# Two halved weight differences, two later roundings, weights' work ahead of finished tiles, and the last squares summed on VectorE

## The chip, the cores and the metric

The kernel runs on one core of a Trainium2 chip. The metric is device time in microseconds (us) of one execution. Five engines run beside each other, each in its own program order: TensorE (PE, with its weight loads PEld), VectorE (DVE), ScalarE (ACT), GpSimd (POOL) and SyncE (SP), which here only issues transfers. They hand work to one another by semaphores.

## The reference

A decoder trunk of two layers on 1024 tokens of width 1024, batch 1, all in float32. Layer 0 mixes tokens with a recurrent block (RG-LRU), layer 1 with stick-breaking attention; each mixer is followed by a feed-forward part with `D_FF` = 2816. What is computed around the change:

```python
def rms_norm(x, g):
    xf = x.astype(jnp.float32)
    y = xf * lax.rsqrt(jnp.mean(xf * xf, axis=-1, keepdims=True) + RMS_EPS)
    return (y * g.astype(jnp.float32)).astype(x.dtype)

def swiglu_ffn(x, w_in, w_out):
    gu = jnp.einsum("bsd,df->bsf", x, w_in)
    h = jax.nn.silu(gu[..., :D_FF]) * gu[..., D_FF:]
    return jnp.einsum("bsf,fd->bsd", h, w_out)

    # per layer
    hn = rms_norm(h, mix_norm[layer])
    h = h + mixed                      # the mixer's output for hn
    h = h + swiglu_ffn(rms_norm(h, ffn_norm[layer]), ffn_w_in[layer], ffn_w_out[layer])
    # after both layers
    return rms_norm(h, final_norm)
```

## The kernel before

**Operands in two parts.** To keep float32 accuracy each operand is split into a high part, rounded by ScalarE to TensorE's `fp32r` format, and a low part, the difference, made by VectorE. One matrix product is then three matmuls (lines 142 to 144): high weights by high data, high weights by low data, low weights by high data. A low part of the weights is so first read by the third matmul of a product.

**Layout.** Activations lie transposed: tile `h[d][n]` holds 128 of the 1024 features (d is 0 to 7) by 512 of the 1024 tokens (n is 0 or 1).

**Seven products.** The feed-forward parts are done by a Strassen-like scheme: a 2 by 2 block product with seven smaller products instead of eight, in the order `ORDER = (0, 1, 2, 3, 4, 6, 5)`. The seven weight operands are made from the raw weights by VectorE sums (`s12`, `s2`, `s3`, `do_s4`) and splits: `a_hi`/`a_lo` (tiles `wah`, `wal`, products 0 and 1), `b_hi`/`b_lo` (`wbh`, `wbl`, products 2 and 4), `c_hi`/`c_lo` (`wch`, `wcl`, products 3 and 5), `d_hi`/`d_lo` (`wd`, product 6). The `_hi` step is on ScalarE, the `_lo` step on VectorE. The seven products lie in three PSUM banks: products 0, 2, 4 and 5 share one, 3 and 6 another. A product that comes on top of an earlier one in its bank (`onto`) may start only after the earlier one has been copied out.

**Steps.** A loop over `steps` runs first 21 "f" steps (columns of `ffn_w_in`, results gated by SiLU and stored through memory) and then the 13 "v" steps, the *visits* of `ffn_w_out`: visit (d, p0, p1) adds pairs p0 to p1 of the inner features to the four tiles of features d and d+4. Visits 9 to 12 are the last for d = 1, 2, 3, 0. Inside a step the loop index `k` runs over the seven products. After each product, in program order: `post` or `post_out` takes the product from PSUM (products 0, 2, 3 and 4 of a visit by a ScalarE copy, line 1176, and then a VectorE add or subtract, lines 1178 and 1180; the others by VectorE straight from PSUM); then the tiles that the product before has finished are worked up by `finished`; then the weight work of this and of the next step (`c_hi`, `c_lo` at k = 0; `d_hi`, `d_lo`, the next step's `a_hi` at 2; its `s12` at 3; `a_lo`, `s2`, `s3` at 4; `b_hi`, `do_s4` at 5). `b_lo` opens the next step. A prologue (lines 993 to 1022) computes column 0 and makes the weights of step 1.

**What `finished` does.** In layer 0 (not `final`) it stores the tile, splits it for the next mixer (`prep`: ScalarE line 220, VectorE line 221) and squares it for the next norm (`squares`: ScalarE line 216, sum by VectorE line 217). In layer 1 (`final`) it squares the tile on ScalarE (line 216; the first square of each n goes straight into `acc[n]`, line 213), adds the square on GpSimd (line 217), and scales the tile by the final norm's gain on ScalarE (line 227). The square goes through `rbc[n]`, one buffer for each n. `finish` (from line 1386) then runs visit 12 of layer 1 for single tiles, sums the squares by matmuls with a column of ones (`stats`, line 206), and transposes, scales and stores the output.

**Roundings of the visits' data.** The moving operands of the visits come back from memory in one part and are split by `split_op` (ScalarE line 1113, VectorE line 1114). A list `tasks` says after which product of the last f step (0 to 6) or of the first visit (7 is its first product) each split is issued:

```python
tasks = [(at, p, i) for at, i in zip((2, 2, 3, 4, 5, 5, L), ORDER) for p in range(2)]
```

**Order.** In both feed-forward blocks the order on TensorE, ScalarE, VectorE and GpSimd is the order of the code (`manual_schedule`); only SyncE's queue is ordered by the planner there. In the attention all five queues follow the code.

Of the kernel before, what the change touches and what calls it, by code (L numbers as in the profile page):

```python
# [33 lines left out]
def trunk(  # L34
# [21 lines left out]
    nc = tc.nc  # L56
    f32 = lambda t: t.bitcast(F32)
# [40 lines left out]
    rbc = [cp.tile([P, NB], F32, name=f"rbc{n}") for n in range(NH)]  # L98
    acc = [None] * NH
# [12 lines left out]
    def load_raw(src, shape):  # L112
        raw = rp.tile([P, D], F32, tag="raw", name="raw")
        view = raw if len(shape) == 1 else raw.rearrange("p (a b) -> p a b", a=shape[0])
        nc.sync.dma_start(view, src)
        return raw
# [33 lines left out]
    def wtile(nm):  # L150
        return wpool[0].tile([P, D], F32R, tag="w", name=nm)
# [59 lines left out]
    def squares(h, d, n, sqp, acc, eng=None, first=None):  # L211
        if d == 0 if first is None else first:
            nc.scalar.square(acc[n], h[d][n])
        else:
            sq = sqp[n % len(sqp)] if isinstance(sqp, list) else sqp.tile([P, NB], F32, tag="sq", name="sq", bufs=2)
            nc.scalar.square(sq, h[d][n])
            (eng or nc.gpsimd).tensor_add(acc[n], acc[n], sq)

    def prep(h, d, n, gcol):
        nc.scalar.activation(xh[d][n], h[d][n], AF.Copy, scale=vc[:, gcol + d : gcol + d + 1])  # L220
        nc.vector.scalar_tensor_tensor(
            xl[d][n], h[d][n], vc[:, gcol + d : gcol + d + 1], f32(xh[d][n]), op0=ALU.mult, op1=ALU.subtract
        )


    def gain(h, d, n):
        nc.scalar.activation(h[d][n], h[d][n], AF.Copy, scale=vc[:, V_FIN + d : V_FIN + d + 1])
# [31 lines left out]
    with ExitStack() as st, tc.manual_schedule(engines={E.PE, E.Activation, E.DVE, E.Pool, E.SP}):  # L259
# [95 lines left out]
        for ks in (range(4), range(4, ND)):  # L355
            for lhs, rhs in ((0, xh), (0, xl), (1, xh)):
                for k in ks:
                    first, last = lhs == k == 0 and rhs is xh, lhs == 1 and k == ND - 1
# [35 lines left out]
    with ExitStack() as st:  # L394
        lp = st.enter_context(tc.tile_pool(name="lp", bufs=1, reuse_waits="tile"))
        psl.append(lst.enter_context(tc.tile_pool(name="psB", bufs=2, space=PSUM, reuse_waits="tile")))
        V = nc.vector
        lam = vc[:, V_LAM : V_LAM + ND]
        sm = lambda name: lp.tile([P, ND], F32, name=name)
        V = nc.vector  # L400
# [164 lines left out]
    ORDER = (0, 1, 2, 3, 4, 6, 5)  # L565
    BANK = {0: 0, 2: 0, 4: 0, 5: 0, 1: 1, 3: 2, 6: 2}
    HK = ND // 2
# [57 lines left out]
    def mix_out_ffn_in(mix, bias, layer, gnext, outs):  # L625
        w_in = ffn_w_in[layer]
        gcol = V_FFN + layer * ND
        V = nc.vector
# [5 lines left out]
        v, h = {}, []  # L634
# [10 lines left out]
        if outs:  # L645
# [6 lines left out]
            class Six:  # L652
                at = 0
# [14 lines left out]
        class Weights:  # L668
# [14 lines left out]
            def part(self, t, x):  # L683
                return half(t, x)[:, 0 : self.m * P]
# [22 lines left out]
                self.wa = wtile("wah")  # L707
                nc.scalar.copy(self.full(self.wa), self.full(self.ra))

            def a_lo(self):  # L710
                lo = wtile("wal")
                V.tensor_sub(self.full(lo), self.full(self.ra), self.full(f32(self.wa)))
                self.put((0, 1), self.wa, lo)

            def b_hi(self):
# [38 lines left out]
        def weights_in(f, now=True):  # L754
            w = Weights(lambda x: load_raw(cols(w_in, x * DFF + f * P), (ND,)))
            if now:
                w.load_a()
                w.load_b()
            return w
# [11 lines left out]
        with tc.manual_schedule(engines={E.PE, E.Activation, E.DVE, E.Pool}):  # L771
# [12 lines left out]
            for j in range(HK):  # L784
                rows = (j, j + HK)
                dn = [(d, n) for d in rows for n in range(NH)] if j else [(d, n) for n in range(NH) for d in rows]
                for k, (d, n) in enumerate(dn):
                    o = HK * j + k
                    if (d, n) in begun:
                        ps = begun[d, n]  # L790
                        hi, lo = mix.w[d]
# [24 lines left out]
                    elif o == 14:  # L816
                        w.b_hi()
                        w.b_lo()
                        nw = weights_in(1)
# [28 lines left out]
            def post0(i, ps):  # L848
                g0, g1, u0, u1 = halves(0)
                if i == 0:  # L850
                    nc.scalar.copy(g1, ps)
                elif i == 1:
                    V.tensor_add(g0, ps, g1)
                elif i == 2:
                    V.tensor_add(g1, ps, g1)
                elif i == 4:
                    V.tensor_add(u0, ps, g1)
                elif i == 3:
                    V.tensor_sub(u1, u0, ps)
                    V.tensor_sub(g1, g1, ps)  # L860
                elif i == 5:
                    V.tensor_add(u0, ps, u0)
                else:
                    V.tensor_sub(g1, g1, ps)
# [131 lines left out]
            for k, i in enumerate(ORDER0[:6]):  # L996
                part(P0[i], w, i, rhs_in[i], (HK - 1,))
                if k == 1:
                    w.d_hi()
                    w.d_lo()  # L1000
                elif k == 3:
                    nw.a_hi()
                elif k == 5:
                    nw.a_lo()
                if k < 5:
                    post0(i, P0[i])
            ps = half(ob, 0)
# [107 lines left out]


            L = NPROD
            tasks = [(at, p, i) for at, i in zip((2, 2, 3, 4, 5, 5, L), ORDER) for p in range(2)]

# [28 lines left out]


            begun_sq, last_sq = set(), []
            done = []

            def finished(d, n):
                if final:
                    squares(h, d, n, rbc, acc, first=n not in begun_sq)
                    gain(h, d, n)
                else:
                    nc.sync.dma_start(hd[d][n], h[d][n])  # L1160
                    prep(h, d, n, gnext)
                    if d in (VISITS[-1][0], VISITS[-2][0], VISITS[-1][0] + HK, VISITS[-2][0] + HK):
                        last_sq.append((d, n))
                    else:
                        squares(h, d, n, acc, rbc, V, first=n not in begun_sq)
                begun_sq.add(n)
# [25 lines left out]
            for s_, (kind, x) in enumerate(steps):  # L1192
                w, nw, ahead = nw, nxt, None
# [23 lines left out]
                for k, i in enumerate(ORDER):  # L1217
# [18 lines left out]
                    if not final and kind == "v" and x == NV - 1:  # L1236
                        if k == 0:
                            raw = load_raw(cols(w_qkv, 0), (ND,))
                        elif k == 4:
                            qh = ring.four.tile([P, D], F32R, tag="w", name="whi")  # L1240
                            nc.scalar.copy(qh, raw)
                        elif k == 5:
                            ql = ring.four.tile([P, D], F32R, tag="w", name="wlo")
                            V.tensor_sub(ql, raw, f32(qh))
                            k3 = lambda t: t.rearrange("p (k c) -> p k c", k=ND)
                            wq0.append((k3(qh), k3(ql)))
                    if i == 1 and even:
                        ga, gb = (q4(halves(x)[0], y) for y in range(2))
                        V.tensor_add(ga, I[0], ga)
                        V.tensor_add(ga, I[1], ga)  # L1250
                        inner_w()
                    elif i == 1 and odd:
                        ha, hb = (q4(halves(x)[0], y) for y in range(2))
                        V.tensor_sub(gb, gb, I[3])
                        V.tensor_add(ha, I[0], ha)
                        V.tensor_add(hb, I[0], hb)
                        V.tensor_sub(hb, hb, I[2])
                        V.tensor_add(ha, I[1], ha)
                    elif kind == "f":
                        post(x, i, banks[b])  # L1260
                        if i == 3 and even:
                            V.tensor_sub(gb, gb, I[2])
                            V.tensor_add(gb, I[0], gb)
                    else:
                        old = done[:]
                        del done[:]
                        post_out(x, i, banks[b])
                        for dn in old:
                            finished(*dn)
                    if s_ == 0:  # L1270
                        if k < 2:
                            for _ in range(2):
# [6 lines left out]
                    if k == 0:  # L1279
                        if kind == "v":  # L1280
                            w.c_hi()
                        w.c_lo()
                    elif k == 2:
                        w.d_hi()
                        w.d_lo()
                        if nw:
                            nw.a_hi()
                    elif nw and last_two:
                        if k == 4:
                            nw.a_lo()  # L1290
                            nw.r_hi()
                        elif k == 6:
                            nw.r_lo()
                    elif nw:
                        if k == 3:
                            nw.s12()
                        elif k == 4:
                            nw.a_lo()
                            nw.s2()
                            nw.s3()  # L1300
                        elif k == 5:
                            nw.b_hi()
                            nw.do_s4()
                    soon = kind == "f" and x + 1 in PAIRS
                    if soon and k == 3:
                        inner_sums(nw.ra, ahead.ra)
# [63 lines left out]
                        open_last()  # L1370
            for dn in done:
                finished(*dn)
            last_sq.sort(key=lambda t: t[1])
            for k, (d, n) in enumerate(last_sq):
                nc.scalar.square(acc[k % NH], h[d][n])
# [102 lines left out]
    with ExitStack() as st:  # L1478
# [261 lines left out]
        with tc.manual_schedule(engines={E.PE, E.Activation, E.DVE, E.Pool, E.SP}):  # L1740
# [3 lines left out]
            first = qkv_steps(0)  # L1744
# [20 lines left out]
            c = 0  # L1765
# [84 lines left out]
```

## Time and profile before

| what | value |
|---|---|
| median of three runs (lowest, highest) | 2173.48 us (2171.96, 2173.48) |
| time of the profiled execution | 2172.33 us |
| its span, first to last instruction | 2170.6 us |
| ScalarE busy | 1110.1 us (51%) |
| VectorE busy | 1777.2 us (82%) |
| GpSimd busy | 122.0 us (6%) |

The time of an execution is 1.7 us more than the span of its trace. Stretches that the text speaks of, in us from the span's start:

| stretch | where |
|---|---|
| 333 to 343 | prologue of layer 0's feed-forward part (1542 in layer 1) |
| 746, 1946 | last f step to visit 0, layer 0 and layer 1 |
| 932 | visit 10 to visit 11, layer 0 |
| 954 | layer 0's last visit to the first q/k/v product |
| 2129 | visit 10 to visit 11, layer 1 |
| 2144.5 to 2170.6 | `finish` |

A line of the timeline reads: start (us), length (us), engine, source line, operation, output tile <- input tiles, shapes, count, and in brackets how long the engine had been idle and for whom it waited. A line of the waits reads: engine, tile and line <- the engine and line waited for: us in total, times, longest. Lines of grouped instructions give a count and shortest, median and longest duration in ns.

### The profile page before, as it was taken

Reading aid. Unit: us, or ns where it says so; the run is one execution under the profiler, and the core shown is the slowest. Engines: PE = TensorE matmul, PEld = TensorE weight load, DVE = VectorE, ACT = ScalarE, POOL = GpSimd, SP = SyncE. Lnnn points to the kernel's source line nnn. Section 1 sums busy time; section 2 is a strip of 40 time slices with the busy share of each in tenths; the row PEclk is TensorE's granted clock in tenths of the full one; section 3 lists DMA queues with packets and bytes.
Section 4 is the critical chain, followed back from the end, with each engine's and each line's share of the span. In section 5 each row is a group of like instructions: output and inputs, shape, how many; then the busy total and the mean of one; then the engine's idle time right before and its main releaser. Section 6 shows DMA issues by size and latency. Waiting matters only on the chain.

```text
span 2170.6 us, 28348 instructions
## 1 busy us (share of the span) xinstructions
PE 2157.1 (99%) x10414; PEld 1812.1 (83%) x10414; DVE 1777.2 (82%) x2604; ACT 1110.1 (51%) x1821; POOL 122.0 (6%) x85
## 2 busy tenths in 40 slices
PE   8999999999999999999999999999999999999998
PEld 7888888888888888888888888888888888888887
DVE  7888778888888887887888888876888888888886
ACT  6577445444444544554555555553544444454556
POOL 1222020000000000000000000012000000000002
PEclk9999999999999999999999999999999999999999
DMA  7111422334445864434333344553133444587442
GB/s 234 49 49 39 163 87 72 107 126 160 134 149 201 267 222 130 146 119 104 99 97 93 95 105 107 147 202 119 60 120 113 153 141 156 176 276 232 136 154 89
DMA packets 305323, 294.49 MB, mean 136 GB/s; under 512 B 16280, under 2 KB 212000, under 8 KB 305184
## 3 DMA queue, kind: packets, MB, share of 16 engines
q1 hardware_dynamic: 305024, 292.42, 42.8%
q8 instruction: 81, 1.33, 0.2%
q14 instruction: 58, 0.48, 0.1%
q10 hardware_dynamic: 160, 0.27, 0.0%
HBM read 184.09 MB, written 83.36 MB: 123 GB/s over the span
## 4 chain that ended last, share of the span: by engine, by line
PE 97%; DVE 2%; ACT 1%; issue 0%; DMA 0%; DVEq 0%; ACTq 0%
PE p_ps L144 17%; PE p_ps L142 17%; PE p_ps L143 17%; PE qk_ps L142 4%; PE qk_ps L144 4%; PE qk_ps L143 4%; PE wt_ps L1654 3%; PE a_ps L143 3%; PE a_ps L144 3%; PE a_ps L142 3%; PE ob_ps L143 3%; PE ob_ps L142 3%; PE ob_ps L144 2%; PE z_ps L1620 2%; PE av_ps L1676 2%; PE z_ps L1621 2%
## 5 line engine op out<-in xcount | busy, mean ns | idle before, releaser
L142 PE MATMUL p_ps<-vh,wbh 128*128 128x512 f32 x524 | 204.8, 391 | 0.0
L143 PE MATMUL p_ps<-vl,wbh 128*128 128x512 f32 x524 | 204.5, 390 | 0.0
L144 PE MATMUL p_ps<-vh,wbl 128*128 128x512 f32 x524 | 204.2, 390 | 0.2 <-DVE wbl L721 0.2
L142 PE MATMUL p_ps<-vh,wch 128*128 128x512 f32 x524 | 204.2, 390 | 0.0
L144 PE MATMUL p_ps<-vh,wcl 128*128 128x512 f32 x524 | 204.1, 390 | 0.0
L143 PE MATMUL p_ps<-vl,wch 128*128 128x512 f32 x524 | 203.9, 389 | 0.0
L717 ACT CAST wbh<-sb 128x1024 fp32r<-128x1024 f32 (+2 forms) x69 | 69.6, 1008 | 191.6 <-DVE sb L701 191.6
L1633 ACT ACTIVATE w<-z_ps 128x128 f32<-128x128 f32 (+1 forms) x192 | 94.1, 492 | 143.1 <-PE z_ps L1621 143.0
L144 PE MATMUL p_ps<-vh,wal 128*128 128x512 f32 x396 | 154.3, 390 | 0.1
L143 PE MATMUL p_ps<-vl,wah 128*128 128x512 f32 x396 | 154.1, 389 | 0.0
L142 PE MATMUL p_ps<-vh,wah 128*128 128x512 f32 x396 | 154.1, 389 | 0.0
L1664 DVE TENSOR_TENSOR tl<-wt_ps,th 128x512 fp32r<-128x512 f32 x192 | 97.9, 552 | 68.0 <-ACT th L1663 67.9
L144 PEld LDWEIGHTS p_ps<-vh,wbl 128*128 128x128 f32 x524 | 98.4, 188 | 22.3 <-DVE wbl L721 1.5
L144 PEld LDWEIGHTS p_ps<-vh,wcl 128*128 128x128 f32 x524 | 98.4, 188 | 21.1 <-DVE wcl L731 0.6
L142 PEld LDWEIGHTS p_ps<-vh,wch 128*128 128x128 f32 x524 | 98.4, 188 | 20.4 <-ACT tb L1176 0.2
L143 PEld LDWEIGHTS p_ps<-vl,wch 128*128 128x128 f32 x524 | 98.4, 188 | 20.4
L142 PEld LDWEIGHTS p_ps<-vh,wbh 128*128 128x128 f32 x524 | 98.6, 188 | 19.2 <-ACT ta L1176 0.2
L143 PEld LDWEIGHTS p_ps<-vl,wbh 128*128 128x128 f32 x524 | 98.6, 188 | 18.6
L142 PE MATMUL qk_ps<-vh,whi 128*128 128x512 f32 x264 | 111.2, 421 | 0.0
L1640 DVE TENSOR_TENSOR_SCAN w<-w,unit 128x128 f32<-128x128 f32 (+3 forms) x128 | 103.7, 816 | 4.6 <-ACT w L1633 4.3
L144 PE MATMUL qk_ps<-vh,wlo 128*128 128x512 f32 x264 | 103.7, 393 | 0.0
L143 PE MATMUL qk_ps<-vl,whi 128*128 128x512 f32 x264 | 103.4, 392 | 0.0
(390 smaller groups left out, 5896.4 us busy)
## 6 DMA issues: line engine op xcount, KB each, us to landing
raw<-in_ffn_w_in SPq DMA_DIRECT2D x88, 512.0 KB, 3.9
vl<-pd SPq DMA_DIRECT2D x128, 256.0 KB, 3.5
pd<-U SPq DMA_DIRECT2D x90, 256.0 KB, 2.3
kk<-two SPq DMA_DIRECT2D x64, 256.0 KB, 4.1
raw<-in_ffn_w_out SPq DMA_DIRECT2D x56, 256.0 KB, 3.6
raw<-in_attn_w_qkv SPq DMA_DIRECT2D x24, 512.0 KB, 4.0
h<-hd SPq DMA_DIRECT2D x32, 256.0 KB, 5.4
hd<-h SPq DMA_DIRECT2D x32, 256.0 KB, 2.0
```

What stands on the lines that cost most here:

```text
L142: nc.tensor.matmul(ps, lhsT=wh, rhs=mh, start=first, stop=False, **kw)
L143: nc.tensor.matmul(ps, lhsT=wh, rhs=ml, start=False, stop=False, **kw)
L144: nc.tensor.matmul(ps, lhsT=wl, rhs=mh, start=False, stop=last, **kw)
L717: nc.scalar.copy(self.full(self.wb), self.full(self.sb))
L1620: nc.tensor.matmul(ps[:, 0 : c1 - c0], lhsT=lhsT, rhs=KK[q][hx][:, 0, c0:c1], start=True, stop=False)
L1621: nc.tensor.matmul(ps[:, 0 : c1 - c0], lhsT=lhsT, rhs=KK[q][hx][:, 1, c0:c1], start=False, stop=True)
L1633: nc.scalar.activation(F, ps[:, 0:n], AF.Sigmoid, scale=-SC)
L1640: nc.vector.tensor_tensor_scan(rev, rev, unit[:, NB - n :][:, ::-1], 0.0, op0=ALU.mult, op1=ALU.add)
L1654: nc.tensor.transpose(tp[:, c : c + P], W[q, hx, j, kb // 4][:, (kb % 4) * P : (kb % 4 + 1) * P], ident)
L1664: nc.vector.tensor_sub(tl[:, q0:], tp[:, q0:], f32(th)[:, q0:])
L1676: nc.tensor.matmul(ps[:, q0:], lhsT=VV[q][:, kb, hx], rhs=tl[:, q0:], start=False, stop=last)
```

## The change

Four things are edited. `a_lo` gets a form that makes `wal` by two instructions of half the width, used once in each prologue, and the first low q/k/v weights `wlo` at the end of layer 0 are made in two instructions, feature tiles 1, 2, 5, 6 first and 0, 3, 4, 7 second. The splits for product 6 move from after the sixth product of the last f step (5) to after the first of visit 0 (`L`, 7), those for product 5 from there to one product later. `finished` moves behind the weight work of the same product. In layer 1 the sums of squares go from GpSimd to VectorE, a product after the square (`add_up`).

```diff
-            def a_lo(self):
+            def a_lo(self, parts=1):
                 lo = wtile("wal")
-                V.tensor_sub(self.full(lo), self.full(self.ra), self.full(f32(self.wa)))
+                if parts == 1:
+                    V.tensor_sub(self.full(lo), self.full(self.ra), self.full(f32(self.wa)))
+                else:
+                    for x in range(2):
+                        V.tensor_sub(self.part(lo, x), self.part(self.ra, x), self.part(f32(self.wa), x))
                 self.put((0, 1), self.wa, lo)
...
                 elif k == 5:
-                    nw.a_lo()
+                    nw.a_lo(2)
...
-            tasks = [(at, p, i) for at, i in zip((2, 2, 3, 4, 5, 5, L), ORDER) for p in range(2)]
+            tasks = [(at, p, i) for at, i in zip((2, 2, 3, 4, 5, L, L + 1), ORDER) for p in range(2)]
...
-            done = []
+            done, to_add = [], []
+
+            def add_up():
+                while to_add:
+                    n = to_add.pop(0)
+                    V.tensor_add(acc[n], acc[n], rbc[n])
 
             def finished(d, n):
                 if final:
-                    squares(h, d, n, rbc, acc, first=n not in begun_sq)
+                    if n in begun_sq:
+                        nc.scalar.square(rbc[n], h[d][n])
+                        to_add.append(n)
+                    else:
+                        nc.scalar.square(acc[n], h[d][n])
                     gain(h, d, n)
...
                             ql = ring.four.tile([P, D], F32R, tag="w", name="wlo")
-                            V.tensor_sub(ql, raw, f32(qh))
                             k3 = lambda t: t.rearrange("p (k c) -> p k c", k=ND)
+                            ka = lambda t: t.rearrange("p (a k c) -> p a k c", a=2, k=HK)
+                            for y in (slice(1, 3), slice(0, HK, HK - 1)):
+                                V.tensor_sub(ka(ql)[:, :, y], ka(raw)[:, :, y], ka(f32(qh))[:, :, y])
                             wq0.append((k3(qh), k3(ql)))
...
                         post_out(x, i, banks[b])
-                        for dn in old:
-                            finished(*dn)
                     if s_ == 0:
...
                             nw.b_hi()
                             nw.do_s4()
+                    if kind == "v":
+                        add_up()
+                        for dn in old:
+                            finished(*dn)
                     soon = kind == "f" and x + 1 in PAIRS
...
             for dn in done:
                 finished(*dn)
+                add_up()
             last_sq.sort(key=lambda t: t[1])
```

## The prediction

> **What bounds the kernel now.** First the page's engine rows, then PEld's waits, then the timeline of each place that is edited.
>
> ```profile
> PE 2157.1 (99%) x10414; PEld 1812.1 (83%) x10414; DVE 1777.2 (82%) x2604; ACT 1110.1 (51%) x1821; POOL 122.0 (6%) x85
> ```
> ```profile
> PEld p_ps L144 <- DVE wbl L721: 1.5, 3, 0.7
> PEld p_ps L144 <- DVE wal L712: 1.0, 2, 0.5
> ...
> PEld p_ps L142 <- ACT ta L1176: 0.7, 2, 0.5
> PEld p_ps L144 <- DVE wcl L731: 0.6, 2, 0.4
> ...
> PEld qk_ps L144 <- DVE wlo L1244: 0.4, 1, 0.4
> ```
>
> TensorE is the bound everywhere, so an edit pays only where TensorE waits. All waits that the edits can reach are these 4.2 us of its weight loads. How much of such a wait TensorE itself loses is read from the first prologue:
>
> ```profile
> 342.61 0.39 PE L142 MATMUL p_ps<-vh,wah 128*128 128x512 f32 x1
> 342.84 0.39 PE L143 MATMUL p_ps<-vl,wah 128*128 128x512 f32 x1
> 343.29 0.50 PE L144 MATMUL p_ps<-vh,wal 128*128 128x512 f32 x1
> 343.63 0.40 PE L142 MATMUL p_ps<-vh,wah 128*128 128x512 f32 x1
> ```
>
> Matmuls start 0.23 apart; here one comes 0.45 after its predecessor and the next 0.34 after that. So 0.22 is lost to the wait and 0.11 to picking up again, 0.33 of a wait that the list counts as 0.5: two thirds. The 4.2 us are therefore worth 2.8 us at most, 0.13% of the kernel, and whatever the change adds is set against that.
>
> **Halves of `wal`: -0.7.** The difference starts too late for the third matmul of step 1:
>
> ```profile
> 342.02 1.22 DVE L712 TENSOR_TENSOR wal<-raw,wah 128x1024 fp32r<-128x1024 f32 x1
> ```
>
> The first half, which alone product 0 reads, takes the 0.69 of a 512-wide VectorE row (below) and ends at 342.71, before the 343.07 at which the third matmul is due. The second is read 12 matmuls after 342.61, at 345.3, and is there by 343.4. Both waits go: two thirds of 1.0. Two instructions for one keep VectorE 0.06 longer (starts 0.60 apart, twice, for 1.14), which no wait behind it sees.
>
> **Halves of `wlo`: -0.3.** The q/k/v product begins with features 1, 5, 2, 6, which the first half holds; the second half has some 12 matmuls of cover. Two thirds of 0.4.
>
> **Roundings two products later: +0.1 in all.** Before visit 0 of layer 1 (and alike in layer 0):
>
> ```profile
> 1943.13 2.50 DVE L1114 TENSOR_TENSOR vl<-vl,vh 128x512 fp32r<-128x512 f32 x4
> 1945.54 0.69 DVE L721 TENSOR_TENSOR wbl<-sb,wbh 128x512 fp32r<-128x512 f32 x1
> ...
> 1949.81 0.43 DVE L740 TENSOR_TENSOR wd<-s,wd 128x256 fp32r<-128x256 f32 x1
> ```
> ```profile
> 1944.53 0.59 ACT L1176 COPY U<-p_ps 128x512 f32<-128x512 f32 x1 [0.23 <-PE p_ps L144]
> ```
> ```profile
> 1946.29 0.50 PE L144 MATMUL p_ps<-vh,wbl 128*128 128x512 f32 x1
> ...
> 1950.54 0.39 PE L144 MATMUL p_ps<-vh,wd 128*128 128x512 f32 x1
> ```
>
> Two of the four splits leave the place ahead of `wbl`, which starts 1.2 earlier; its wait (0.4 of the 1.5 in each layer) goes, -0.27 a layer. They then stand with the two of product 5 ahead of `wd`. VectorE cannot use the whole 1.2, as its next instruction needs the copy that ends at 1945.12: it starts at 1945.15 instead of 1946.14, 1.0 earlier. Two splits of 0.60 more come behind it, so `wd` ends at 1950.24 + 0.2 = 1950.45. TensorE, 0.25 earlier without the first wait, wants it at 1950.29. It loses 0.05 (from a result to its reader, 1946.23 to 1946.29 at `wbl`) + 0.16 + 0.11 = 0.32. Net +0.05 a layer; bounds -0.27 (the end of `wd` is hidden) to +0.3.
>
> **Weights ahead of finished tiles, layer 0: +0.2.** `finished` now waits behind `b_hi` on ScalarE, which itself waits for the sums:
>
> ```profile
> 929.20 0.84 ACT L717 CAST wbh<-sb 128x768 fp32r<-128x768 f32 x1 [0.56 <-DVE sb L701]
> ```
> ```profile
> 933.28 0.96 DVE L721 TENSOR_TENSOR wbl<-sb,wbh 128x768 fp32r<-128x768 f32 x1
> ```
> ```profile
> 934.46 0.39 PE L144 MATMUL p_ps<-vh,wbl 128*128 128x512 f32 x1
> ```
>
> ScalarE is then free for visit 10's tile (6, 1) at 929.94 (0.74 after `b_hi` starts) and has split it 0.72 later, at 930.66. VectorE, which went straight from the take-over of product 6 (done at 929.68) to that tile, has only the short sum `do_s4` (0.47) to do meanwhile and stands still from 930.15 to 930.70. All behind inherits the 0.55: `wbl` starts at 933.83 and ends at 934.79. TensorE wants it at 934.46: 0.38 with the hand-over, and 0.11 to pick up, +0.49. In return `wcl` of visit 11 no longer stands behind tile (6, 0): its wait of 0.4 goes, -0.27. Bounds: -0.27 to +0.5. Before visit 10 the same move is hidden (the VectorE instruction ahead of `wbl` waits for TensorE), before visit 12 there are no squares. The stores of finished tiles on SyncE's queue wait for the tile alone, and its loads run two steps ahead: nothing.
>
> **Sums on VectorE, layer 1: +1.8.** What they replace:
>
> ```profile
> L217 POOL TENSOR_TENSOR acc<-acc,rbc x30: 1289/1302/1747, 274.1 to 2146.2; 128x512 f32<-128x512 f32 x30
> L217 DVE TENSOR_TENSOR acc<-acc,rbc x8: 684/686/689, 348.7 to 1551.5; 128x512 f32<-128x512 f32 x8
> ```
> ```profile
> 2128.33 1.66 DVE L701 TENSOR_TENSOR sb<-raw 128x384 f32<-128x384 f32 x1
> ...
> 2132.18 1.93 DVE L721 TENSOR_TENSOR wbl<-sb,wbh 128x768 fp32r<-128x768 f32 x1
> 2134.03 1.79 DVE L1180 TENSOR_TENSOR g<-ta,g 128x512 f32<-128x512 f32 x1
> ```
> ```profile
> 2131.28 0.63 ACT L216 ACTIVATE rbc<-g 128x512 f32<-128x512 f32 x1 [0.42 <-DVE g L1178]
> 2131.95 0.73 ACT L227 ACTIVATE g<-g,vc 128x512 f32<-128x512 f32 x1
> 2132.57 0.57 ACT L1176 COPY ta<-p_ps 128x512 f32<-128x512 f32 x1
> ```
> ```profile
> 2133.22 0.48 PE L142 MATMUL p_ps<-vh,wbh 128*128 128x512 f32 x1
> ```
>
> Ten sums of 1.3 on GpSimd become ten of 0.69 on VectorE. The gain: beside GpSimd's sum `wbl` takes 1.93, in layer 0 0.96; without it the waits for `wbl` (0.7) and for the copy `ta` (0.7) could go, 0.9 in all. The loss: squares of tiles with the same n share `rbc[n]`. At the end of visit 10 the tiles (6, 1) and (2, 1) come one product apart. The second square must wait for the first's sum, and that now stands on VectorE behind the take-over of the last product. VectorE reaches that take-over, which stood 0.60 ahead of `wbl`, at 2131.07 instead of 2131.58: `s3` (line 701) no longer takes 1.66 beside GpSimd but some 0.55, less one sum of 0.60 put in. The sum runs from 2131.67 to 2132.36, the square starts at 2132.42, the gain follows 0.67 later and the copy of product 0 of visit 11 another 0.63 later, at 2133.72 instead of 2132.57; it ends at 2134.31. Product 2 lies on product 0's bank and was due at 2133.22: it starts at 2134.37, +1.15, and +0.11. It lost some 0.6 around `wbl` already and product 6 0.3 at `ta`, both of which go (ScalarE has caught up by product 3). TensorE enters `finish` 0.15 late at this point.
>
> There the same hand-over meets the norm:
>
> ```profile
> 2144.73 0.69 DVE L1180 TENSOR_TENSOR g<-p_ps,g 128x512 f32<-128x512 f32 x1 [1.36 <-PE p_ps L144]
> ```
> ```profile
> 2146.85 1.28 ACT L1438 ACT_TABLE_LOAD   x1
> 2148.14 0.20 ACT L1438 ACTIVATE rcol<-ones 128x1 f32<-128x1 f32 x1
> ```
> ```profile
> 2151.56 0.69 DVE L1408 TENSOR_TENSOR acc<-acc,rbc 128x512 f32<-128x512 f32 x1 [0.70 <-ACT rbc L1406]
> ```
> ```profile
> 2152.48 0.61 PE L206 MATMUL st_ps<-ones,acc 128*128 128x1 f32 x5
> ```
>
> From the last take-over T (2144.73) to `stats` there are 7.75. Now: take-over and `wrl` 0.60 each, sum of (7, 1) 0.75 with its hand-over, then on ScalarE square and gain of (3, 1) and of (7, 0), 2 x (0.67 + 0.63), table 1.28, root 0.11: `finish`'s first square starts at T + 5.94. Square 0.66, its sum 0.60, the second tile's take-over 0.75, its square 0.70, its sum 0.75: `stats` at T + 9.40, 1.65 late. With the 0.15: +1.8, and nothing behind `stats` gives it back, since TensorE's transposes follow in order. Bounds: -0.9 (all hidden) to +3.1 (one more late copy, 1.26). I take 1.8, as every length is from a row of the same 20 us.
>
> A page of the Trainium skill would make this longer: "ScalarE: Activation LUTs", section "What ACT_TABLE_LOAD costs", gives 1.28 us for the load and about 1.38 us for a drain with each switch of sets. The row has the 1.28, and the root starts at its end, with no drain in sight; by the page's figure the term would be an estimated +3.2 and the total +2.5.
>
> **Sum.** -0.7 - 0.3 + 0.1 + 0.2 + 1.8 = +1.1 us. The execution profiled took 2172.33 (span 2170.6 and 1.7 around it): 2173.4. The median, 2173.48, is 1.15 above that execution, so I forecast 2174.6, no change that this kernel's measurement can tell (0.2%, 4.3 us).
>
> **The rivals.** *The gains alone.* If ScalarE's late copy and `finish`'s sums are covered after all, nothing is lost: -2.8, 2170.7. For it: every wait of the list is on a moved or shortened instruction. Against: one `rbc[n]`, and 0.2 between the end of the sum that `stats` reads (2152.25) and `stats`. *The halves don't count.* If a reader waits for the whole tile, the 1.0 of the halves is not won: 2175.6. Against: `wcl` is made and read in halves already. *The late copy again.* Products 3 and 4 of visit 11 wait for their copies like product 0, another 1.26 each: 2177.1. For it: `ta` and `tb` are in the wait list. Against: by product 3 ScalarE has 0.6 to spare. *A slower table switch.* If the switch first lets the last square and gain run out, 1.30 is added to the chain in `finish`: 2175.9. Against: the load's row starts where the last gain ends (2146.85). (A drain as on the Trainium skill's "ScalarE: Activation LUTs" would be such a wait.) *The other side: the clock falls.* TensorE's granted clock:
>
> ```profile
> 2169.00:2170.00 1.00, 0.00 (x0) 0.00 (x0) 0.00 (x0) 0.00 (x0) 0.00 (x0) 0.61 0.02 4
> ```
>
> The last matmul ends near 2165; four us later the clock, 1.00 until then, drops. If the wait at 2133 or at `stats` let it drop, TensorE's remaining 13 to 31 us would run at half speed: up to as much again, 2187 to 2205. It decides from a wait of about four us. Against: my longest is 1.65. (The Trainium skill, "TensorE: Matmul & The Clock Gate", "What's actually happening", puts the limit at one idle window of about 3.4 us; by that rule too the clock stays.)
>
> **How the numbers follow.** Forecast 0.46; gains alone 0.19; halves don't count 0.10; late copy again 0.13; table switch 0.05; clock 0.07. The forecast's own bounds: 2172.9 to 2176.5. The range goes down to 2170.5 and up to 2177.3, which leaves out the clock, half of the late copy and some of the gains. Slower by over 0.2% (above 2177.8) are the clock and 0.06 of the late copy, where it comes with the upper bounds of the other terms: 0.13. Faster by over 0.2% (below 2169.1) is more than all waits are worth: 0.03, for waits that I don't see. The rest, 0.84, is within 0.2%.
>
> **What would show it.** Right: no wait of PEld for `wal` and `wlo`; no 1.93 on `wbl`; before visit 11 of layer 1 a wait for the copy `ta` of about 1.2; `stats` starting 9.4 after the last take-over, with a wait for VectorE's `acc`; a short wait for `wd` in visit 0 and for `wbl` before visit 11 of layer 0. Wrong: ScalarE's copy of product 0 on time, or `stats` without a wait. A drop of the granted clock before 2165 would be the last rival.

## The result and the profile after

The changed kernel takes 2176.32 us (median of 22 runs, 2173.55 to 2177.0), the kernel before on the same chips 2172.84 (22 runs, 2171.85 to 2174.35): a ratio of 1.0015, with an interval of 1.0009 to 1.0022. It is 3.5 us slower, inside the range that I gave and 1.7 above the forecast, still within the 0.2% of "same". The profiled execution took 2176.84 us, its span is 2175.1.

The engine row of the page, and the list of PEld's waits (us in total, times, longest):

```profile
PE 2159.7 (99%) x10414; PEld 1815.5 (83%) x10414; DVE 1780.3 (82%) x2617; ACT 1109.3 (51%) x1821; POOL 107.1 (5%) x75
```
```profile
PEld st_ps L206 <- DVE acc L1426: 1.7, 1, 1.7
...
PEld p_ps L142 <- ACT ta L1189: 1.3, 1, 1.3
...
PEld p_ps L144 <- DVE wd L744: 0.7, 2, 0.3
PEld p_ps L144 <- DVE wbl L725: 0.7, 1, 0.7
...
PEld st_ps L206 <- DVE rbc L1394: 0.5, 1, 0.5
```

`wal`, `wlo` and `wcl` are gone from the list. In their place stand `acc` at `stats`, one long wait for the copy `ta`, two short ones for `wd`, one for `wbl` (layer 0), and two kinds that I had not named: for `rbc` at another `stats`, and three for a copy `G` (0.9 in all, 0.3 before).

Since TensorE issues the same matmuls in the same order in both kernels, I laid the two traces side by side and noted each place where the distance between a matmul's two starts changes. A step includes what TensorE loses in picking up again behind a wait, some 0.1. Steps below 0.05 are left out; the others add up to the difference of the spans to within 0.1:

| place (us in the trace before) | predicted | measured |
|---|---|---|
| start-up, to 13 us | - | +1.25 |
| 343, 1542: halves of `wal` | -0.33 each | -0.34 each |
| 746, 1946: `wbl` no longer waits | -0.27 each | -0.25 each |
| 751, 1951: product 6 late | +0.32 each | +0.30 each |
| 934: `wbl` late, layer 0 | +0.49 | +0.51 |
| 937: `wcl` no longer waits, layer 0 | -0.27 | -0.23 |
| 955: halves of `wlo` | -0.3 | -0.26 |
| 966: second `stats` of the attention | none | +0.30 |
| 2133 to 2141: visit 11, layer 1, net | +0.15 | +0.15 |
| 2152: `stats` in `finish` | +1.65 | +1.74 |
| 2154 to 2158: granted clock | none | +1.58 |
| total | +1.1 | +4.5 |

The first row is no effect of the edits. The 16 transposes that open both traces are unchanged:

```profile
9.55 1.96 PE L316 MATMUL tp<-ident,xt 128*128 128x128 f32 x16 [1.47 <-DVE hc L323]
```
```profile
9.70 3.65 PE L316 MATMUL tp<-ident,xt 128*128 128x128 f32 x16 [1.69 <-DMA xt<-in_x]
```

The first row is of the kernel before, the second of the changed one: there this execution met TensorE at half speed for longer. In the traces of the experiments this step goes either way, from -0.8 to +1.6, which fits runs of one kernel that differ by 2 us or more. Without it 3.2 of the 4.5 us are left, and the medians differ by 3.5.

**The +0.30 at 751 and 1951 is two waits.** In the changed kernel near 1951:

```profile
1946.62 2.18 ACT L1117 CAST vh<-vl 128x512 fp32r<-128x512 f32 x4
...
1950.22 0.59 ACT L1189 COPY G<-p_ps 128x512 f32<-128x512 f32 x1
...
1950.86 0.50 PE L142 MATMUL p_ps<-vh,wd 128*128 128x512 f32 x1
...
1951.50 0.50 PE L144 MATMUL p_ps<-vh,wd 128*128 128x512 f32 x1
```

The moved splits have a half on ScalarE too. It now rounds four tiles at once where it had rounded two (2.18 for 1.14), its next copies are late, and product 6 waits for the copy `G` that ends at 1950.81: 0.03 and 0.11 for picking up. The difference `wd` costs 0.08 and 0.11.

**The two large steps are where the prediction had put them.** Visit 10 to visit 11 of layer 1, from the timeline of the changed kernel:

```profile
2132.72 0.68 DVE L1162 TENSOR_TENSOR acc<-acc,rbc 128x512 f32<-128x512 f32 x1
2133.32 0.95 DVE L725 TENSOR_TENSOR wbl<-sb,wbh 128x768 fp32r<-128x768 f32 x1
...
2133.43 0.63 ACT L1167 ACTIVATE rbc<-g 128x512 f32<-128x512 f32 x1 [0.74 <-DVE acc L1162]
2134.10 0.72 ACT L227 ACTIVATE g<-g,vc 128x512 f32<-128x512 f32 x1
2134.73 0.56 ACT L1189 COPY ta<-p_ps 128x512 f32<-128x512 f32 x1
...
2135.34 0.50 PE L142 MATMUL p_ps<-vh,wbh 128*128 128x512 f32 x1 [0.91 <-ACT ta L1189]
```

The sum (line 1162) frees `rbc`; only then does ScalarE, 0.74 idle, start the second square, then the gain, then the copy for which TensorE stands still. And `wbl` takes 0.95 instead of 1.93, as GpSimd works on nothing beside it. In `finish`:

```profile
2145.89 0.69 DVE L1193 TENSOR_TENSOR g<-p_ps,g 128x512 f32<-128x512 f32 x1 [1.35 <-PE p_ps L144]
...
2150.49 1.28 ACT L1456 ACT_TABLE_LOAD   x1
2151.79 0.20 ACT L1456 ACTIVATE rcol<-ones 128x1 f32<-128x1 f32 x1
...
2154.54 0.69 DVE L1426 TENSOR_TENSOR acc<-acc,rbc 128x512 f32<-128x512 f32 x1 [0.69 <-ACT rbc L1424]
...
2155.28 1.05 PE L206 MATMUL st_ps<-ones,acc 128*128 128x1 f32 x8 [1.48 <-DVE acc L1426]
```

From the last take-over (2145.89) to `stats` (2155.28) there are 9.39 us. I had worked out 9.40.

**What I had not expected follows from that wait.** Three stretches of 3.41 us, the first beginning where TensorE's last matmul ahead of the wait ends (length, then busy time of PE and the other engines, then the granted clock, PEclk):

```profile
2153.80:2157.22 3.42, 1.94 (x18) 1.94 (x18) 1.91 (x8) 2.43 (x5) 0.00 (x0) 1.00 0.00 0
2157.22:2160.63 3.41, 3.41 (x19) 3.41 (x17) 2.50 (x6) 2.26 (x4) 0.00 (x0) 0.50 0.31 117
2160.63:2164.04 3.41, 3.41 (x33) 3.41 (x33) 1.57 (x8) 1.92 (x5) 0.00 (x0) 1.00 0.51 191
```

In the first TensorE is idle for 1.48. In the second, back at work, it is granted half its clock: 19 matmuls instead of some 33. In the third the clock is whole again. Half of 3.41 is 1.71, and the matmuls fall back 1.58.

### The profile page after: what moved, and what is told of

Read it like the earlier page. It is cut to its first block, busy times and chain, and to the rows that moved or that the text cites. A ratio compares the mean times of both kernels' runs of the same rounds, so it can differ in the third digit from the quotient of the medians.

```text
span 2175.1 us, 28346 instructions
## 1 busy us (share of the span) xinstructions
PE 2159.7 (99%) x10414; PEld 1815.5 (83%) x10414; DVE 1780.3 (82%) x2617; ACT 1109.3 (51%) x1821; POOL 107.1 (5%) x75
## 4 chain that ended last, share of the span: by engine, by line
PE 97%; DVE 1%; ACT 1%; DMA 0%; issue 0%; SPq 0%; DVEq 0%
PE p_ps L142 17%; PE p_ps L143 17%; PE p_ps L144 17%; PE qk_ps L142 4%; PE qk_ps L144 4%; PE qk_ps L143 4%; PE wt_ps L1672 3%; PE a_ps L143 3%; PE a_ps L144 3%; PE a_ps L142 3%; PE ob_ps L144 3%; PE ob_ps L143 3%; PE ob_ps L142 3%; PE z_ps L1638 2%; PE av_ps L1694 2%; PE z_ps L1639 2%
```

## The experiments

Four questions were open: whether the shared square buffer, rather than VectorE's load, makes the chain late; whether the clock falls because of the wait at `stats`, and from what length; where the 0.30 at 966 comes from; and what the order in layer 0 costs.

### Who pays for the late sums

**The sums back on GpSimd**, all else as changed:

```diff
-                    if n in begun_sq:
-                        nc.scalar.square(rbc[n], h[d][n])
-                        to_add.append(n)
-                    else:
-                        nc.scalar.square(acc[n], h[d][n])
+                    squares(h, d, n, rbc, acc, first=n not in begun_sq)
```

> The changed kernel with layer 1's sums of squares back on GpSimd; halves, roundings and the order of the finished tiles stay as changed. Theory (the sums on VectorE make the late copy before visit 11 and the wait at stats, and that wait lets the clock fall): no wait of the stats matmuls for acc, granted clock 1.00 until the end, about 1.6 + 1.7 us less than the changed kernel, near 2173.0, the same as the kernel before within 0.5 us. Rival (it is the moved order, not the sums): the wait at stats and the half clock stay, 2175.5 or more.

**The sums on VectorE, each square in a buffer of its own** (four free halves of the `UT` tiles in turn), all else as changed:

```diff
-                    n = to_add.pop(0)
-                    V.tensor_add(acc[n], acc[n], rbc[n])
+                    n, sq = to_add.pop(0)
+                    V.tensor_add(acc[n], acc[n], sq)
...
-                        nc.scalar.square(rbc[n], h[d][n])
-                        to_add.append(n)
+                        sq = half(UT[1 + n_sq[0] // 2 % 2], n_sq[0] % 2)
+                        n_sq[0] += 1
+                        nc.scalar.square(sq, h[d][n])
+                        to_add.append((n, sq))
```

> The changed kernel, sums still on VectorE, but each square goes to one of four buffers of its own, so that no square waits for an earlier sum. Theory (the hand-over through one rbc[n] is what costs): no wait of about 1.1 for the copy ta before visit 11, wait at stats under 0.3, clock 1.00: 1.1 + 1.6 + 1.7 less than the changed kernel, near 2171.9, about 1 us faster than the kernel before. Rival (VectorE has too little room for ten more sums): at least half of the wait at stats stays, clock falls as before, 2175 or more.

GpSimd: 2172.19 us (2170.89 to 2172.97, 11 runs), 0.9994 of the kernel before (0.9985 to 1.0003). Own buffers: 2172.07 (2170.77 to 2172.86, 11 runs), 0.9991 (0.9982 to 1.0000). After 2125 us the list of PEld's waits has one line in each, and none for `stats`; first GpSimd's, then that of the own buffers:

```profile
PEld p_ps L142 <- ACT ta L1185: 0.7, 1, 0.7
```
```profile
PEld p_ps L142 <- ACT ta L1191: 0.5, 1, 0.5
```

In both traces the granted clock stays at 1.00 to the last matmul, and visit 11 is a gain: -0.48 net with GpSimd, which fits that kernel's coming out lower than expected, and -0.69 with own buffers, where the changed kernel has +0.15. These are steps of single traces, and the kernel before does not lose the same there each time: in one of the experiments below (the second trace with two subtractions, whose visit 11 is unedited) it is 0.61 faster. There GpSimd's sum took 2.82 instead of 1.75, and VectorE's line 701 beside it 0.55 instead of 1.66. VectorE does the same ten sums in the second kernel as in the changed one, and the wait at `stats` is gone. So it is not their load that cost the time, but one buffer handed to and fro between two engines that each work in order. Ten sums on VectorE with room for the squares are as good as ten on GpSimd; the two kernels cannot be told apart.

### What makes the clock fall

**TensorE kept busy ahead of `stats`**, by matmuls into a PSUM bank whose result nothing reads; first twelve of 256 columns, later six of 512 (the diff is of the six):

```diff
-        rest = last(1, *mid, ahead=lambda: stats(acc[0], pp, "p", 0))
+        def filled():
+            ps = pp.tile([P, NB], F32, tag="p", name="st_ps")
+            for _ in range(FILL):
+                nc.tensor.matmul(ps, lhsT=w.a[0][0][:, 0:P], rhs=R[p0][0][0], start=True, stop=True)
+            for i in range(4):
+                nc.tensor.matmul(ps[:, i : i + 1], lhsT=acc[0][:, i * P : (i + 1) * P], rhs=ones, start=True, stop=True)
+            rstd(rcol[:, 0:4], ps[:, 0:4])
+
+        rest = last(1, *mid, ahead=filled)
```

> The changed kernel with twelve matmuls of 256 columns (about 1.4 us) put ahead of the stats matmuls, into unused columns, so that TensorE works through most of its wait. Theory (the idle time lets the clock fall): stats starts where it did, the granted clock stays 1.00 until the end, 1.7 us less than the changed kernel, near 2174.6. Rival (the clock falls for what follows, the many small matmuls and transposes, and not for the wait): half clock for some 3.4 us after stats all the same, 2176.3.

> The changed kernel with six 512-wide matmuls on a spare PSUM bank put on TensorE ahead of `stats` (nothing reads them), so that TensorE does not stand still while it waits for the sum. It repeats the twelve narrower ones with half as many instructions. Theory (the clock falls because TensorE stood still at `stats`): clock 1.00 to the last matmul, and the time is the changed kernel's less 1.7: 0.9993 of it, about 1.0007 of the kernel before (2174.6). Rival (the clock falls because the eight narrow matmuls come late, whatever stands before them): half clock for some 3.4 us stays, 1.0015. With half the extra instructions the last stores should land as early as in the changed kernel; if what delayed them with twelve fillers comes again, the trace ends about 1.9 later than its last matmul says, 1.0009 or more.

Twelve: 2175.73 us (2174.94 to 2176.69, 11 runs), 1.0009 (1.0000 to 1.0018). Six: 2175.34 (2174.53 to 2176.45, 11 runs), 1.0008 (0.9999 to 1.0017). With six, the stretch with the wait and the one behind it:

```profile
2152.83:2156.25 3.42, 3.33 (x24) 2.73 (x22) 1.97 (x6) 2.43 (x5) 0.00 (x0) 1.00 0.00 0
2156.25:2159.66 3.41, 3.41 (x33) 3.41 (x32) 2.71 (x9) 2.11 (x4) 0.00 (x0) 1.00 0.29 109
```

TensorE is idle for 0.09 and the clock stays whole. `stats` is as late as in the changed kernel (+1.64), yet behind it only the 0.10 for picking up is lost. By the ratios the kernel with matmuls that do nothing is 0.0007 faster than the changed one, some 1.5 us, where 1.7 had been expected. The intervals of 1.0008 and 1.0015 overlap, so the traces carry this, not the times. With twelve the trace shows the same, but its last stores landed 1.8 later than the last matmul led one to expect. With six they did not, and the times of the two kernels cannot be told apart, which fits a matter of that one execution. What it was stays open.

**The same wait without the change**: the kernel before, with idle subtractions on VectorE ahead of the sum that `stats` reads.

```diff
                 nc.scalar.square(sq, t)
+                if (x, n, i0) == (1, 0, 0):
+                    for _ in range(DOSE):
+                        nc.vector.tensor_sub(rows[4][:, 0:NB], sq, t)
                 if add:
```

> The kernel before with one idle VectorE subtraction (0.60) put ahead of the sum that `stats` reads, nothing else. `stats` waits some 0.4 us. Theory (a still TensorE ahead of `stats` lets the clock fall, from some length between 0.4 and 1.5 us): no fall here, +0.4 to +0.5, ratio 1.0002. Rival (any wait there lets it fall): +2.1, 1.0010.

> As with one subtraction, but two: `stats` waits some 1.0 us. If the clock falls the time is +1.1 and another 1.7, 1.0013; if not, +1.1, 1.0005. The theory leaves this length open.

> As before, but three: `stats` waits some 1.6 us, as long as in the changed kernel. Theory (the length of the stand-still does it, whatever the change is): half clock for some 3.4 us from two us after the wait, +1.6 and +1.7 = +3.3, ratio 1.0015. Rival (the clock falls in the changed kernel for another reason, such as what its earlier waits did): +1.6 alone, 1.0007.

> The kernel before with two idle VectorE subtractions ahead of the sum that `stats` reads, a second look at the same kernel. The granted clock changes on a grid of 3.41 us, and in the first look the stand-still of 0.99 lay across a boundary of it (0.71 and 0.28). If the still share of one stretch of the grid decides, a look in which all 0.99 lie in one stretch may fall to half clock for the next; if 0.99 is too short whatever its place, the clock stays at 1.00.

One subtraction: 2174.21 us, 1.0003 (0.9995 to 1.0012). Two: 2175.41, 1.0010 (1.0002 to 1.0019). Three: 2176.68, 1.0015 (1.0006 to 1.0024); 11 runs each. With three, as in the changed kernel, the clock falls, here for two stretches on end:

```profile
2151.32:2154.73 3.41, 1.69 (x15) 1.49 (x13) 2.91 (x5) 1.12 (x2) 0.00 (x0) 1.00 0.00 0
2154.73:2158.15 3.42, 3.42 (x17) 3.42 (x18) 1.40 (x8) 1.19 (x3) 0.00 (x0) 0.50 0.00 0
2158.15:2161.56 3.41, 3.41 (x18) 3.41 (x17) 2.05 (x4) 2.19 (x4) 0.00 (x0) 0.50 0.33 124
```

So it is the wait ahead of `stats` that does it, whatever made it. Two traces of the kernel with two subtractions show how. `stats` waits 0.99 both times. The first trace:

```profile
2151.18:2154.60 3.42, 2.69 (x22) 2.46 (x20) 2.47 (x4) 0.94 (x2) 0.00 (x0) 1.00 0.00 0
2154.60:2158.01 3.41, 3.15 (x28) 3.15 (x29) 2.45 (x10) 2.18 (x5) 0.00 (x0) 1.00 0.00 0
2158.01:2161.42 3.41, 3.41 (x33) 3.38 (x32) 2.19 (x6) 2.60 (x7) 0.00 (x0) 1.00 0.60 224
```

And the second trace of the same kernel:

```profile
2154.30 1.05 PE L206 MATMUL st_ps<-ones,acc 128*128 128x1 f32 x8 [0.99 <-DVE acc L1411]
...
2152.96:2156.38 3.42, 2.43 (x21) 2.22 (x21) 2.60 (x8) 1.80 (x4) 0.00 (x0) 1.00 0.00 0
2156.38:2159.79 3.41, 3.41 (x18) 3.41 (x17) 2.35 (x6) 2.19 (x4) 0.00 (x0) 0.50 0.40 150
```

The stretches are on a grid: every change of the clock within a trace lies a whole number of 3.41 us from the others. In the first trace the grid cuts the idle time into 0.73 and 0.26, and the clock stays. In the second all 0.99 lie in one stretch, and the next one runs at half clock: 1.57 lost. Where the grid lies differs from one execution to the next.

### The 0.30 at 966, and layer 0's order

**`wlo` whole again**, all else as changed:

```diff
+                            V.tensor_sub(ql, raw, f32(qh))
                             k3 = lambda t: t.rearrange("p (k c) -> p k c", k=ND)
-                            ka = lambda t: t.rearrange("p (a k c) -> p a k c", a=2, k=HK)
-                            for y in (slice(1, 3), slice(0, HK, HK - 1)):
-                                V.tensor_sub(ka(ql)[:, :, y], ka(raw)[:, :, y], ka(f32(qh))[:, :, y])
```

> The changed kernel with `wlo` at the end of layer 0 made in one piece again. Theory (the halves' gain is given back at the second attention `stats`, since the squares for it on VectorE had only some 0.2 to spare and the halves keep VectorE 0.07 longer): in the trace neither the -0.26 at the first q/k/v product nor the +0.30 at `stats` near 966, so TensorE is 0.04 ahead of the changed kernel from there on. Rival (the 0.30 comes from the moved order in layer 0): the -0.26 goes and the +0.30 stays, 0.26 behind.

**`finished` ahead of the weights' work in layer 0**, behind it in layer 1 alone:

```diff
+                        if not final:
+                            for dn in old:
+                                finished(*dn)
...
-                        for dn in old:
-                            finished(*dn)
+                        if final:
+                            for dn in old:
+                                finished(*dn)
```

> The changed kernel with `finished` ahead of the weights' work in layer 0, as before, and behind it in layer 1 alone. Theory: the +0.51 at `wbl` and the -0.23 at `wcl` near 934 to 938 both go, 0.28 less; the +0.30 at the `stats` near 966 stays, as it hangs on `wlo`. Rival: the +0.30 goes too.

With `wlo` whole neither the -0.26 nor the +0.30 is in the trace (2175.86 us, one run). With the old order in layer 0 the +0.51 and the -0.23 are gone but for -0.05, which is the 0.28 expected net to within 0.05, and the +0.30 stays (2174.99 us, one run). So the halves of `wlo` bring 0.26, and 11 us later it is lost again. The rows, in turn of the kernel before, of the changed one and of the one with `wlo` whole:

```profile
965.27 0.69 DVE L1376 TENSOR_TENSOR rbc<-rbc,acc 128x512 f32<-128x512 f32 x1
...
966.20 0.95 PE L206 MATMUL st_ps<-ones,rbc 128*128 128x1 f32 x8
```
```profile
966.68 0.69 DVE L1394 TENSOR_TENSOR rbc<-rbc,acc 128x512 f32<-128x512 f32 x1
...
967.00 0.39 PE L144 MATMUL qk_ps<-vh,wlo 128*128 128x512 f32 x1
967.42 0.72 PE L206 MATMUL st_ps<-ones,rbc 128*128 128x1 f32 x5
```
```profile
966.33 0.39 PE L144 MATMUL qk_ps<-vh,wlo 128*128 128x512 f32 x1
966.56 0.61 PE L206 MATMUL st_ps<-ones,rbc 128*128 128x1 f32 x5
```

Before, the last sum of squares ends at 965.96 and `stats` comes at 966.20: 0.24 to spare, less 0.05 for the hand-over. TensorE, by now 0.32 earlier (0.26 and small steps behind it), and VectorE, 0.07 later for two instructions instead of one, use up 0.39, which is 0.20 too much. `stats` comes 0.42 after its predecessor instead of 0.23, and the next matmul loses 0.11 more.

The kernel with the old order in layer 0 adds one thing to the clock. Its wait at `stats` is the changed kernel's, and the clock does not fall:

```profile
2154.97 1.05 PE L206 MATMUL st_ps<-ones,acc 128*128 128x1 f32 x8 [1.48 <-DVE acc L1430]
...
2150.84:2154.25 3.41, 2.65 (x22) 2.44 (x20) 1.32 (x3) 2.73 (x6) 0.00 (x0) 1.00 0.00 0
2154.25:2157.66 3.41, 2.69 (x24) 2.69 (x25) 2.45 (x9) 2.04 (x5) 0.00 (x0) 1.00 0.00 0
2157.66:2161.08 3.42, 3.42 (x33) 3.42 (x32) 2.45 (x6) 2.57 (x6) 0.00 (x0) 1.00 0.46 174
```

The grid cuts the 1.48 into 0.76 and 0.72. The traces together, with TensorE's idle time in each stretch of the grid (its length less PE's busy time) and the busy time of the eight one-column matmuls of `stats` that lie in it. The last four rows are stretches away from that wait: one in the attention, and the one in which the last matmul ends:

| kernel | idle in the stretch | one-column matmuls in it | clock of the next |
|---|---|---|---|
| three subtractions | 1.72 | 0.18 | 0.50 |
| changed | 1.48 | 1.05 | 0.50 |
| `wlo` whole | 1.48 | 0.83 | 0.50 |
| two, second trace | 0.99 | 1.05 | 0.50 |
| old order in layer 0 | 0.76, then 0.72 | 0, then 1.05 | 1.00 |
| two, first trace | 0.73, then 0.26 | 0, then 1.05 | 1.00 |
| one subtraction | 0.27 | 1.05 | 1.00 |
| six filling matmuls | 0.09 | 1.05 | 1.00 |
| before | 0 | 0.95 | 1.00 |
| each of the thirteen traces, attention near 1424 | 1.05 or 1.06 | 0 | 1.00 |
| sums back on GpSimd, last matmuls | 1.75 | 0 | 1.00 |
| own buffers, last matmuls | 1.95 | 0 | 1.00 |
| the version from the gains (below), last matmuls | 2.26 | 0 | 0.50 |

Idle time alone does not decide. In the attention TensorE waits 1.06 in one piece, wholly inside one stretch of the grid, and with own buffers it is idle for the last 1.95 of a stretch; the next stretch has its whole clock both times. The rows of the kernel before, then of own buffers:

```profile
1424.01 0.39 PE L1676 MATMUL av_ps<-tl,v 128*128 128x256 f32 x1 [1.06 <-DVE tl L1664]
...
1421.71:1425.12 3.41, 2.35 (x20) 2.15 (x19) 3.41 (x6) 2.29 (x7) 0.00 (x0) 1.00 1.03 393
1425.12:1428.54 3.42, 3.12 (x21) 2.50 (x20) 3.42 (x7) 2.56 (x6) 0.00 (x0) 1.00 0.14 55
```
```profile
2164.18:2167.59 3.41, 1.46 (x14) 1.22 (x12) 2.11 (x7) 1.82 (x3) 0.00 (x0) 1.00 0.90 333
2167.59:2171.01 3.42, 0.00 (x0) 0.00 (x0) 0.00 (x0) 0.00 (x0) 0.00 (x0) 1.00 0.56 210
```

What the waits at `stats` have beside them, and these two have not, are the one-column matmuls. Counted as idle, they put the limit between 1.77 (0.72 + 1.05), where the clock stays, and 1.90 (1.72 + 0.18), where it falls. The 1.95 of own buffers does not fit by 0.05, which may lie in the modelled ends of the matmuls. So this reading is nearer to the traces, but not shown. The second half-clock stretch with three subtractions has no idle time, and 1.56 of one-column matmuls at half speed; whether the clock stays low by the same limit is open.

### A version from the gains

**Halves as changed, own buffers for the squares, `finished` behind the weights in layer 1 alone, roundings as before:**

```diff
-            tasks = [(at, p, i) for at, i in zip((2, 2, 3, 4, 5, L, L + 1), ORDER) for p in range(2)]
+            tasks = [(at, p, i) for at, i in zip((2, 2, 3, 4, 5, 5, L), ORDER) for p in range(2)]
```

The other two edits are those of the own buffers and of the old order in layer 0.

> Halves, own buffers for the squares with the sums on VectorE, finished tiles behind the weights in layer 1 alone, roundings where the kernel before has them. Theory: the halves' gains (-0.9), layer 0's waits around 935 and 967 gone, no wait at visit 11 and at stats, clock 1.00: about 1.6 us faster than the kernel before, near 2171.2. Rival (the gains are taken back by other waits): within 0.5 us of the kernel before.

2172.05 us (2170.61 to 2172.42, 11 runs), 0.9993 of the kernel before (0.9984 to 1.0002), where 2171.2 had been expected. The trace holds -0.34 twice, -0.26 and +0.30, and -0.69 at visit 11: -1.3, and the median is 1.0 lower. The +0.30 at 966 had been expected to go, but it hangs on `wlo`. About 1 us may be had from this change; as the interval reaches 1.0002, that is not shown. The own buffers with everything else as changed give as much.

## Why the prediction was right or wrong

The forecast held: no change by 0.2%, on the slow side. Part of that is luck. The range left a fall of the clock out; the clock did fall, and only because its price is one stretch did the time stay below 2177.3. Step by step:

- **Halves of `wal`**: two thirds of the listed wait, twice. Right to 0.02, with -0.34 for -0.33.
- **Halves of `wlo`**: the gain of 0.26 came, but the step failed where it named the cover. "The second half has some 12 matmuls of cover" holds for TensorE. Next on VectorE come the sums of squares, which had 0.19 to spare; I had not followed VectorE past the edited instruction to the next thing that TensorE reads from it. The halves are worth nothing in sum instead of -0.3.
- **Roundings**: -0.25 and +0.30 a layer, where I had -0.27 and +0.32. The first is right. The second is right in size by luck: I followed only VectorE's half of the splits and gave the whole 0.32 to `wd`. `wd` costs 0.19, and the rest is ScalarE's late copy, which I had put at nothing.
- **Layer 0's order**: +0.51 and -0.23 for +0.49 and -0.27. Right.
- **Sums on VectorE**: the late second square, the late copy and `stats` at T + 9.39 came as forecast. The +0.15 at visit 11 was measured too, but the terms that I gave for it (+1.15, +0.11, -0.6, -0.3) add up to +0.36. Measured were +1.07 for the first two, -0.50 around `wbl`, -0.30 at product 6, and -0.11 at `wcl`, which I had not counted. At `stats` I had left out the 0.10 for picking up. The own buffers show that the cause is the one I gave, the shared `rbc[n]`. The table load is followed by the root after 0.02 (its row at 2151.79), so the longer switch that the Trainium skill's page "ScalarE: Activation LUTs", section "What ACT_TABLE_LOAD costs", led to was rightly left out of the sum.
- **The gains alone, the halves don't count, the late copy again, a slower table switch**: none came. Products 3 and 4 of visit 11 had their copies in time.
- **The clock falls**: this is the step that failed. "It decides from a wait of about four us", and "my longest is 1.65": I took the condition from the end of the trace, where the clock drops four us after the last matmul. But that drop lies on the grid, and in the traces of this case it comes 2.3 to 5.4 after the last matmul; it is no least length of a wait. What the runs showed: a wait of 0.99 ahead of the one-column matmuls of `stats` is enough if it lies in one stretch of the grid, though 1.06 in the attention is not. The price was wrong too, in the other direction: not half speed for the remaining 13 to 31 us, but for one stretch of 3.41, some 1.6. So the rival came with a price eight to twenty times smaller, on top of my forecast. The kernel before at 2172.84, the steps without start-up and clock, 1.63 (0.53 above my +1.1, of it 0.30 at 966 and 0.10 at `stats`), and the clock's 1.58 make 2176.1; 2176.32 was measured.

The Trainium skill, "TensorE: Matmul & The Clock Gate", section "What's actually happening", has the free-running window of 3413 ns that the traces show as 3.41. But it names a whole idle window as what lowers the clock, and by that rule I let the clock stay; here a window with 0.99 of idle time and 1.05 of one-column matmuls did it.

## What to carry to other kernels

Where TensorE is busy without a gap, price a new wait twice: by its length, and by half of the 3.41 us that may follow at half clock. Here 0.99 was enough beside one-column matmuls, and 1.06 beside matmuls of 128 to 384 columns was not. Whether the fall comes depends also on where the wait lies on a grid that differs from one execution to the next, so one profile can miss it. A buffer that two in-order engines hand to and fro makes each wait for the other's whole queue; before moving work between engines, count the buffers, not only the busy time. And a gain ahead of a just-in-time chain is given back at its end: follow the engine that is edited to the next value of it that the bound engine reads.

## What the hardware showed that I had not expected

Half a clock for one stretch of 3.41 us after 0.99 to 1.72 us of idle time beside one-column matmuls in the stretch before, for two stretches in one case, and none where the same 0.99 or 1.48 was cut in two by the grid. None either after 1.06 us of idle time in one stretch of the attention, or 1.95 behind the last transposes. And six idle matmuls of 512 columns, put into the wait, kept the clock at 1.00.
